# Tokens-first operands of the delta and GLA heads: from TensorE transposes to VectorE block transposes and a pass through DRAM

## The chip, the cores and the metric

The kernel runs on one core of a Trainium2 chip. The metric is the device time of one launch in microseconds (us). A core has a TensorE (PE, matmuls; PEld are its weight loads), a VectorE (DVE), a ScalarE (ACT), a GpSimd (POOL) and a SyncE (SP). SP computes nothing here; it issues most of the DMAs, in order, one after the other. All engines run their own instruction stream in order and wait for each other through semaphores.

## The reference

One inference step of two layers over 320 token columns: 256 prompt tokens (one sequence) and 64 sample tokens (8 sequences of 8), model width 2048, all in float32.

```python
# layer 0, per token: one input projection, split into the parts below
proj = x @ w_in
qkv, b_raw, a_raw, z_a, q_b, k_b, v_b, lr_b, z_b = split(proj)
qkv = silu(causal_conv(qkv, width 4))                 # delta heads: 8 heads, 128 wide
q_a = l2norm(q_a) * 128 ** -0.5;  k_a = l2norm(k_a)
beta = sigmoid(b_raw);  g = -exp(a_log) * softplus(a_raw + dt_bias)
# gated delta rule, in chunks (kb = beta * k, G = cumsum g, decay = exp(G_i - G_j))
A   = strict_lower((kb @ k.T) * decay)
sol = solve(A + I, [v * beta, kb * exp(G)])           # unit lower triangular
v_new = u - w @ S;  o = (q * exp(G)) @ S + ((q @ k.T) * decay) @ v_new
S = S * exp(g_last) + (k * exp(g_last - G)).T @ v_new
# GLA: 4 heads (128 keys, 256 values): S_t = diag(exp(gk_t)) S_{t-1} + k_t v_t^T, o_t = S_t^T q_t
x = x + (concat(norm(o_a) * silu(z_a), norm(o_b) * silu(z_b))) @ w_out
# layer 1: x = x + (RG-LRU(conv4(x w_x)) * silu(x w_g)) @ w_out ; then a final rmsnorm
```

The outputs are the tokens of both groups and the new recurrent states.

## The kernel before

**The dense stream.** All large projections are one stream of 30 groups. A group makes 512 output features in four PSUM accumulators `acc`; it runs over 8 weight chunks `wst` of 512 KB (2 slices of the depth each). Every float32 product is three matmuls on rounded parts: `xh*wh`, `xl*wh`, `xh*wl`. I call such a set of three a product; a group has 64 of them. ACT makes `wh` from `wst` (L246), DVE makes `wl` (L247), SP loads `wst` (L212) into three buffers. Features lie on the partitions, tokens on the columns.

Groups 0 to 5 are the delta heads' Q, K, V, V, K, Q (two halves of four heads each; conv taps on DVE, silu on ACT, into tiles `qkv`), 6 to 9 the GLA's q, k, v, v (tiles `gp`), 10 to 13 the gates, then the output projection and layer 1.

**The side work.** What the heads need beside the stream is written as generators in queues `hi`, `lo`, `lo2`, `tails`. After each product `slot()` advances each queue by one `yield`; a table `WAITS` says how many yields lie between two pieces. A scheduler of the language then orders the instructions of each engine by its own costs, so the place of a piece in an engine's stream is not exactly where the generator emitted it. Mentions of order below are of that final stream.

**The delta heads.** A *quad* is four heads over 128 tokens. There are four prompt quads (two halves of the heads, two chunks) and one of the sample tokens. `quad_a` prepares a quad, and it needs k, q and v with tokens on the partitions:

- it turns k, q and v with TensorE, four 128x128 transposes each (L716 `kt`, L725 `qt`, L767 `vt`; `ident` is the identity);
- ACT takes the sums of squares of k and q from PSUM (`junk`, `ss`), POOL and DVE make `nb` (minus beta over the squared norm of k) and `bk`;
- `df`, `gr` (L751) sum gates, ACT makes `dtm` (decay), PE makes `kk` (L773) and `kq` (L785), DVE multiplies them with `dtm` to `bt` and `mt`;
- `nb` is needed along columns too: PE turns it (L795 `nbt`), ACT copies it, POOL writes it to DRAM, ACT's queue reads it back as `bn`.

Then comes the inverse of the triangular matrix: `bt`'s 32x32 diagonal blocks go through DRAM (`bd_scratch`, `ab`), POOL multiplies `ab` by `bn` (L823) and solves (`invert32`, 62 instructions L828 and L830), the results return through `xd_scratch` as `XT` and `xc`. `quad_front` joins blocks (`lp`, `lxt`, `xp` scaled by `nb`), `quad_b` applies the inverse (`y`), makes the output `po` and the state `sn`. The sample quad has 8x8 blocks and inverts on DVE (`invert`); it reads the old states as `st`.

**GLA.** `gla_head` turns two blocks of v and one of k per chunk with TensorE (L1438, L1439 `gvt`), and ACT copies the three from PSUM (`gvk`).

Of the kernel before, what the change touches and what calls it, by code (L numbers as in the profile page):

```python
# [72 lines left out]
def hybrid_step(ctx, tc, x_cols, x_rows, w_head, w_dense, w_small, w_lr, w_gate, par_a, par_b, par_c, gains, last_gain,  # L73
# [9 lines left out]
    nb_d = nc.dram_tensor("nb_scratch", (20, P), F32, kind="Internal").ap()  # L83
# [3 lines left out]
    xt_d = nc.dram_tensor("xt_scratch", (4, P, P), F32, kind="Internal").ap()  # L87

# [25 lines left out]
    hi, lo, lo2, tails = [], [], [], []  # L114
# [27 lines left out]
    def slot0(n_lo=1):  # L142
        advance(hi)
        for _ in range(n_lo):
            advance(lo)
        advance(lo2)
        advance(tails)

# [397 lines left out]

    def evac_conv_a(slot_name, half, part):
# [53 lines left out]
        def after():  # L601
# [3 lines left out]
            if part == 0 and half == 1:  # L605
                hi.append(later(lambda: lo.extend([delta_half(1), delta_sample()])))
        evac.late = late
# [3 lines left out]
    def small_group():  # L611
        acc = bank("smacc")
        for k in range(KT):
            j = 32 * (k % 4)
            pe.matmul(acc[j:j + 32, :NT], smw[:, k, :], ob[k // 4][:, k % 4, :], start=(k < 4), stop=(k >= KT - 4),
                      tile_position=(0, j))
        dve.tensor_mul(sm[:, :NT], acc[:, :NT], rb0)
# [63 lines left out]
    def quad_prompt(half, c):  # L681
# [10 lines left out]
        q.late = c > 0  # L692
        q.on_tag, q.nbuf = "lg", 2
        return q

    def quad_sample():
# [9 lines left out]
        q.late = True  # L706
        q.on_tag, q.nbuf = "bt", 1
        return q

    def quad_a(q, ws, nbuf):  # L710
        U = q.U
        t = lambda nm, shape=[P, 4, P], bufs=nbuf, tag=None: ws.tile(shape, F32, name=nm, tag=tag or nm, bufs=bufs)
        ss = t("ss", [P, 8])
        ps = bank4("kt")
        for u in range(U):
            pe.transpose(ps[:, u, :], q.k(u), ident)  # L716
        q.ktm = t("ktm")
        act.activation(q.ktm, ps, AF.Copy)
        for u in range(U):
            j = t("junk", [P, P], 1)  # L720
            act.activation(j, ps[:, u, :], AF.Square, accum_out=ss[:, u:u + 1])
        yield from wait("quad_a.1")
        ps = bank4("qt")
        for u in range(U):
            pe.transpose(ps[:, u, :], q.q(u), ident)  # L725
        for u in range(U):
            j = t("junk", [P, P], 1)
            act.activation(j, ps[:, u, :], AF.Square, accum_out=ss[:, 4 + u:5 + u])
        q.bk = t("bk", [P, 4])
        q.nb = t("nb", [P, 4])  # L730
        q.nbe = t("nbe", [P, 4])
        sk = ss[:, 0:4]
        pool.tensor_scalar(sk, sk, EPS, None, op0=OP.add)
        pool.tensor_tensor(q.bk, sk, mhalf[:, :4], OP.pow)
        pool.tensor_mul(q.bk, q.bk, beta[:, q.gc:q.gc + 4])
# [8 lines left out]
        yield from wait("quad_a.2")  # L744
        dve.reciprocal(q.nb, sk)
        dve.scalar_tensor_tensor(q.nb, q.nb, -1.0, beta[:, q.gc:q.gc + 4], op0=OP.mult, op1=OP.mult)
# [13 lines left out]
        dve.tensor_mul(dt, dt, q.um[:, None, :].to_broadcast([P, 4, P]))  # L760
        q.eq = ss[:, 4:8]
        dve.tensor_scalar(q.eq, q.eq, EPS, EPS * P, op0=OP.add, op1=OP.mult)
        dve.tensor_mul(q.nbe, q.nb, es[:, q.gc:q.gc + 4])
        yield from wait("quad_a.3")
        ps = bank4("vt")
        for u in range(U):
# [1331 lines left out]
```

## Time and profile before

| | |
|---|---|
| median of 3 runs | 978.75 us (977.84 to 979.34) |
| span of the profiled execution, first to last instruction | 976.7 us |
| the median less that span | 2.05 us |
| busy: PE, DVE, ACT, POOL | 965.7, 695.6, 532.6, 193.4 us |
| PE idle for an operand: largest rows | 1.4 us (`frs`, the end), 1.2 us (`got`), 0.4 and 0.2 us (first weights) |
| mean DMA rate over the span | 179 GB/s |

The page records no time of the profiled execution apart from its span; the span and the median differ by what lies around the first and last instruction. In a row, the busy time is the sum over instructions, "mean ns" is the length of one from its start to its modelled end; matmuls overlap, so the distance between two starts is shorter than the length.

### The profile page before, as it was taken

How to read it: one execution, taken by the hardware profiler on the slowest of the kernel's cores; microseconds unless marked ns; L12 is line 12 of the kernel's file. 1: busy time of each engine (PE TensorE's matmuls, PEld its weight loads, DVE VectorE, ACT ScalarE, POOL GpSimd, SP SyncE). 2: the span in 40 equal slices, each digit the busy share in tenths (PEclk: the TensorE clock that was granted, in tenths of full speed). 3: DMA queues.
4: the chain of work that ended last, by engine and by line, in shares of the span. 5: the costliest groups of instructions: out<-in, count | busy, mean ns of one | idle time of the engine just before them, and what ended most of it. 6: DMA issues, size and time to landing. Idle time of an engine off the chain costs nothing.

```text
span 976.7 us, 18827 instructions
## 1 busy us (share of the span) xinstructions
PE 965.7 (99%) x6945; PEld 949.2 (97%) x6945; DVE 695.6 (71%) x1464; ACT 532.6 (55%) x1088; POOL 193.4 (20%) x343
## 2 busy tenths in 40 slices
PE   9999999999999999999999999999999999999996
PEld 9999999999999999999989999999999999999996
DVE  7498887666545556788658789667969668876763
ACT  7666865447333454866423345348685885333442
POOL 3010128303381011120106124100010000042200
PEclk9999999999999999999999999999999999999998
DMA  9854445534455376444578887655445445678752
GB/s 321 292 176 123 134 131 155 166 109 121 150 154 150 98 235 215 130 125 130 180 251 265 245 246 249 211 154 151 157 117 189 131 127 171 189 229 253 264 168 108
DMA packets 68125, 175.06 MB, mean 179 GB/s; under 512 B 17116, under 2 KB 26096, under 8 KB 67520
## 3 DMA queue, kind: packets, MB, share of 16 engines
q1 hardware_dynamic: 62904, 163.69, 54.5%
q0 software_dynamic: 2720, 8.66, 2.5%
q10 hardware_dynamic: 2408, 1.49, 0.5%
q8 instruction: 55, 0.90, 0.4%
q14 instruction: 38, 0.31, 0.1%
HBM read 159.14 MB, written 14.68 MB: 178 GB/s over the span
## 4 chain that ended last, share of the span: by engine, by line
PE 96%; DVE 2%; issue 0%; DMA 0%; ACT 0%; SPq 0%; POOL 0%; DVEq 0%; ACTq 0%; POOLq 0%
PE acc L380 82%; PE acc L266 3%; PE fbt L309 1%; PE gpo L1495 0%; PE lg L1683 0%; PE lg L1682 0%; PE lg L1684 0%; PE kq L785 0%; PE kk L773 0%; DMA wst<-in_w_head_dram 0%; PE gsn L1259 0%; PE po L971 0%; PE pq L1059 0%; PE sn L1245 0%; PE y L962 0%
## 5 line engine op out<-in xcount | busy, mean ns | idle before, releaser
L380 PE MATMUL acc<-xh,wh 128*128 128x320 f32 x1856 | 579.9, 313 | 0.4 <-ACT wh L233 0.4
L380 PE MATMUL acc<-xl,wh 128*128 128x320 f32 x1856 | 574.0, 310 | 0.0
L380 PE MATMUL acc<-xh,wl 128*128 128x320 f32 x1856 | 573.0, 309 | 0.2 <-DVE wl L247 0.2
L246 ACT ACTIVATE wh<-wst 128x512 fp32r<-128x512 f32 x479 | 279.2, 624 | 301.1 <-PE acc L380 259.5
L247 DVE TENSOR_TENSOR wl<-wst,wh 128x512 fp32r<-128x512 f32 x479 | 333.4, 726 | 150.6 <-ACT wh L246 149.6
L380 PEld LDWEIGHTS acc<-xh,wh 128*128 128x128 f32 x1856 | 348.6, 188 | 3.3 <-issue 1.3
L380 PEld LDWEIGHTS acc<-xl,wh 128*128 128x128 f32 x1856 | 348.6, 188 | 1.1
L380 PEld LDWEIGHTS acc<-xh,wl 128*128 128x128 f32 x1856 | 348.2, 188 | 0.9 <-DVE wl L247 0.4
L588 DVE SCALAR_TENSOR_TENSOR yc<-slab,pa,yc 128x344 f32<-128x344 f32 x72 | 40.6, 576 | 2.8 <-ACT yc L102 2.4
L830 POOL TENSOR_TENSOR xi<-xi,tmp 128x60 f32<-128x60 f32 (+24 forms) x62 | 25.9, 418 | 4.9
L828 POOL TENSOR_TENSOR tmp<-ab,xi 128x60 f32<-128x60 f32 (+24 forms) x62 | 25.1, 404 | 4.8
L1711 POOL MEMSET aa<- 128x32 f32 x4 | 0.6, 161 | 117.7 <-ACT rr L1698 66.7
L1140 POOL TENSOR_TENSOR uvkh<-uvk,uvkh 32x256 fp32r<-32x256 f32 (+1 forms) x8 | 10.8, 1344 | 51.5 <-DVE uvkh L1136 50.6
L1249 DVE SCALAR_TENSOR_TENSOR ust<-ust,es,sn 128x128 f32<-128x128 f32 x64 | 18.2, 338 | 2.8 <-PE sn L1245 2.0
L1145 POOL TENSOR_TENSOR uvm<-uvh,rm 96x512 fp32r<-96x512 f32 x16 | 19.5, 1242 | 2.8 <-PE sn L1245 2.4
L885 POOL TENSOR_TENSOR so<-so,mhalf 128x4 f32<-128x4 f32 x4 | 4.4, 1106 | 74.2 <-DVE so L884 74.2
L266 PE MATMUL acc<-xl,wh 128*128 128x320 f32 (+1 forms) x64 | 18.7, 292 | 0.0
L266 PE MATMUL acc<-xh,wl 128*128 128x320 f32 (+1 forms) x64 | 18.7, 292 | 0.0
L266 PE MATMUL acc<-xh,wh 128*128 128x320 f32 (+1 forms) x64 | 18.6, 291 | 0.0
L592 ACT ACTIVATE qkv<-yc 128x256 f32<-128x256 f32 x24 | 10.0, 415 | 15.8 <-DVE yc L588 15.6
L1263 DVE SCALAR_TENSOR_TENSOR ugt<-ugt,ebs,gsn 128x256 f32<-128x256 f32 x32 | 14.1, 474 | 5.6 <-PE gsn L1259 5.5
L1642 DVE SCALAR_TENSOR_TENSOR yc<-slab,pb,yc 128x344 f32<-128x344 f32 x32 | 17.5, 572 | 0.6 <-ACT yc L1640 0.5
(464 smaller groups left out, 1057.1 us busy)
## 6 DMA issues: line engine op xcount, KB each, us to landing
wst<-in_w_dense_dram SPq DMA_DIRECT2D x237, 512.0 KB, 4.0
st<-in_state_delta_dram SPq DMA_DIRECT2D x8, 512.0 KB, 6.3
st<-in_state_gla_dram SPq DMA_DIRECT2D x4, 1024.0 KB, 6.9
ust<-in_state_delta_dram SPq DMA_DIRECT2D x8, 512.0 KB
out_s_delta_dram<-ust POOLq DMA_DIRECT2D x8, 512.0 KB, 5.1
ugt<-in_state_gla_dram SPq DMA_DIRECT2D x8, 512.0 KB, 5.6
out_s_gla_dram<-ugt POOLq DMA_DIRECT2D x8, 512.0 KB, 4.2
xtok<-in_x_rows_dram SPq DMA_DIRECT2D x6, 512.0 KB, 5.4
```

Of the source, the lines that this page charges most:

```text
L246: act.activation(h, wst[i][:, a, :], AF.Copy)
L247: env["last_split"] = dve.tensor_sub(l, wst[i][:, a, :], h.bitcast(F32))
L266: mm = pe.matmul(accs[f][:, cols], w[:, fs], x[:, cols], start=(k == 0 and j == 0), stop=(k == KT - 1 and j == 2), skip_group_check=True)
L380: mm = pe.matmul(o, (h, h, l)[j][:, fs], (xh, xl, xh)[j][k], start=(k == 0 and j == 0), stop=(k == KT - 1 and j == 2))
L588: dve.scalar_tensor_tensor(y[:, :n], xp[:, j:j + n], pa[:, ft, j:j + 1], y[:, :n], op0=OP.mult, op1=OP.add)
L828: behind(pool.tensor_mul(tv, ab[:, j, j + 1:, None].to_broadcast([P, m, w]), xi[:, j:j + 1, :w].to_broadcast([P, m, w])))
L830: behind(pool.tensor_add(xi[:, j + 1:, :w], xi[:, j + 1:, :w], tv))
L1140: pool.tensor_sub(o, t[rows, :, cols], o.bitcast(F32))
L1145: pool.tensor_mul(m, src.bitcast(F32)[:, None, :].to_broadcast([R, 4, P]), rm4[:R, :, None].to_broadcast([R, 4, P]))
L1249: dve.scalar_tensor_tensor(s_, s_, es[:, col:col + 1], ps[:, b, :], op0=OP.mult, op1=OP.add)
L1263: dve.scalar_tensor_tensor(s_, s_, ebs[:, h, 4 * hb + b + i:4 * hb + b + i + 1], ps[:, i * 256:(i + 1) * 256], op0=OP.mult, op1=OP.add)
L1642: dve.scalar_tensor_tensor(y[:, :n], xp[:, j:j + n], pb[:, ft, 2 + j:3 + j], y[:, :n], op0=OP.mult, op1=OP.add)
```

## The change

1. Delta k, q and v are no longer turned on TensorE. `turn` lets DVE transpose 32x32 blocks of a whole `qkv` tile (four instructions of 128x256, or 128x128 for the sample tokens) into an `ob` tile, reading every fourth column; SP writes the tile to DRAM (`tp_scratch`, `ts_scratch`), and `load_turned` reads a quad's operand in one DMA with tokens on the partitions (`kin`, `qin`, `rv`). A new queue `turns` holds this work. It is done once per tile, in the groups after the tile is made.
2. `ACT` copies `kin` into `ktm` and takes the squares from SBUF. In half 0 v arrives late, in half 1 q; a generator `rest` in `lo2` fetches the late operand, and `delta_half` holds its `quad_front` until it is there.
3. `nb` stays on partitions: it is multiplied into `dtm` (four instructions per quad in place of one). The transposes `nbt`, the DRAM trip of `nb`, the POOL product L823 and the scaling by `nb` in `quad_front` go; there the copies `xp` are split between DVE and ACT.
4. The blocks of both quads of a half go out together (4 transfers in place of 8) and come back in 5 in place of 10. `bt` of the two quads is one tile.
5. The sample quad loads its first two states after the blocks of its inverse, and the next two after the first `pq`.
6. GLA's v is turned the same way (`gvv`); only k is turned on TensorE.
7. The `WAITS` numbers are changed around all of this.

```diff
-    "small_work.1": 0, ... "quad_a.1": 2, "quad_a.2": 8, ... "quad_a.7": 9, "invert32.1": 18,
+    "small_work.1": 0, ... "quad_a.1": 10, "quad_a.2": 2, ... "quad_a.7": 2, "delta_half.2": 4, "invert32.1": 12,
...
+    def turn(src, d, flag, to, gate):
+        while gate not in env["done"]:
+            yield
+        n = src.shape[2] // P
+        to = to.rearrange("p f t -> p (f t)")[:, :4 * P * n].rearrange("p (c x) -> p c x", c=n)
+        for f in range(4):
+            behind(dve.transpose(to.rearrange("p c (b u j) -> p u c b j", u=4, j=32)[:, f],
+                                 src[:, f, :].rearrange("p (c i b) -> p c b i", c=n, b=4)))
+            yield from wait("turn.1")
+        yield from wait("turn.2")
+        behind(sp.dma_start(d.rearrange("c p x -> p c x"), to))
+        yield from wait("turn.3")
+        env["done"].add(flag)
+
+    def load_turned(out, d, c=0):
+        sp.dma_start(out.rearrange("p a u j -> p a (u j)"), d[c].rearrange("(a i) (b x) -> (i b) a x", a=4, b=4))
...
     def quad_a(q, ws, nbuf):
-        ps = bank4("kt")
-        for u in range(U):
-            pe.transpose(ps[:, u, :], q.k(u), ident)
-        q.ktm = t("ktm")
-        act.activation(q.ktm, ps, AF.Copy)
...
-        ps = bank4("qt")
-        for u in range(U):
-            pe.transpose(ps[:, u, :], q.q(u), ident)
...
+        kin = rows("kin", "mt")
+        load_turned(kin, *turned(1))
+        late = {0: 2, 1: 0}.get(half)
+        if late != 0:
+            qin = q.bt.rearrange("p u (a j) -> p u a j", j=32)
+            load_turned(qin, *turned(0))
+        if late != 2:
+            q.rv = rows("rv")
+            load_turned(q.rv, *turned(2))
...
-        dve.tensor_mul(dt, dt, q.um[:, None, :].to_broadcast([P, 4, P]))
+        q.ktm = t("ktm")
+        act.activation(q.ktm.rearrange("p u (a j) -> p a u j", j=32), kin, AF.Copy)
...
+        for u in range(U):
+            dve.scalar_tensor_tensor(dt[:, u, :], dt[:, u, :], q.nb[:, u:u + 1], q.um, op0=OP.mult, op1=OP.mult)
...
-        ps = bank4("vt")
-        for u in range(U):
-            pe.transpose(ps[:, u, :], q.v(u), ident)
-        q.rv = t("rv")
-        scaled4(q.rv, ps, q.bk, NA0)
...
-        ps = bank("nbt")
-        pe.transpose(ps[:4, :P], q.nb, ident)
-        nbt = t("nbt", [4, P], 1)
-        act.activation(nbt, ps[:4, :P], AF.Copy)
-        pool.dma_start(nb_d[q.id:q.id + 4, :], nbt)
...
     def invert32(ws, first):
-        act.dma_start(bn, bass.AP(tensor=nb_d.tensor, ...))
-        pool.tensor_mul(ab, ab, bn[:, None, :].to_broadcast([P, n, n]))
...
     def delta_sample():
+            yield from quad_a(q, ws, 1)
+            inverse = invert(ws, 4, 8)
+            next(inverse)
+            yield from wait("delta_sample.9")
             load(0)
             load(1)
-            yield from quad_a(q, ws, 1)
-            yield from invert(ws, 4, 8)
+            yield from inverse
...
     def gla_head(h, ws, vt):
-            for hf in range(2):
-                vt = 2 * h + hf
-                pe.transpose(pt[:, hf, :], env["VB", vt // 4][:, vt % 4, cs], ident)
-            pe.transpose(pt[:, 2, :], kd[128][:, cs], ident)
+            pe.transpose(pt[:, :P], kd[128][:, cs], ident)
```

How the streams change is shown at three places. The first is PE where `quad_a` of the first half stands, in group 3. Before, each quad brings its own block of turns and products:

```order
L751 MATMUL df<-ug,sl_r 128x512 x2
L767 MATMUL vt<-ident,qkv 128x128 x4
L773 MATMUL kk<-qkv 128x128 x4
L785 MATMUL kq<-qkv 128x128 x4
L795 MATMUL nbt<-ident,nb 4x128
L380 MATMUL acc<-xh_116,wh 128x320
```

In the changed kernel the same place on PE holds no turn, and both quads' products follow each other:

```order
L788 MATMUL df<-ug,sl_r 128x512
L788 MATMUL gr<-ug,ones_r 128x512
L382 MATMUL acc<-xl_132,wh 128x320
L382 MATMUL acc<-xh_116,wh 128x320
L382 MATMUL acc<-xh_117,wh 128x320
L382 MATMUL acc<-xl_133,wh 128x320
L382 MATMUL acc<-xh_117,wl 128x320
L825 MATMUL kk<-qkv 128x128 x4
L832 MATMUL kq<-qkv 128x128 x4
L825 MATMUL kk<-qkv 128x128 x4
L832 MATMUL kq<-qkv 128x128 x4
```

The turns are gone, and with them the `kt` and `qt` blocks 16 to 20 products earlier; nothing else is added to PE's stream.

The second is DVE at the same moment, up to the first evacuations of group 3 (`slab`). Before:

```order
L742 TENSOR_TENSOR ug<-umask,gth 128x512
L742 TENSOR_TENSOR ug<-umask,gtl 128x512
L760 TENSOR_TENSOR dtm<-dtm,umask 128x512
L111 TENSOR_TENSOR rv<-vt,bk 128x256
L775 TENSOR_TENSOR bt<-kk,dtm 128x512
L788 TENSOR_TENSOR mt<-kq,dtm 128x512
L760 TENSOR_TENSOR dtm<-dtm,umask 128x512
L958 TENSOR_TENSOR eg<-eg,qkv 128x512
L247 TENSOR_TENSOR wl<-wst,wh 128x512 x2
L479 TENSOR_TENSOR slab<-acc,rb_84 128x256
```

In the changed kernel, with the last block transposes of V ahead of it:

```order
L558 STREAM_TRANSPOSE ob_137<-qkv 128x8x32
L249 TENSOR_TENSOR wl<-wst,wh 128x512 x2
L776 TENSOR_TENSOR ug<-umask,gth 128x512
L776 TENSOR_TENSOR ug<-umask,gtl 128x512
L816 SCALAR_TENSOR_TENSOR dtm<-dtm,nb,umask 128x128 x6
L826 TENSOR_TENSOR bt<-kk,dtm 128x512
L816 SCALAR_TENSOR_TENSOR dtm<-dtm,nb,umask 128x128
L835 TENSOR_TENSOR mt<-kq,dtm 128x512
L1006 TENSOR_TENSOR eg<-eg,qkv 128x512
L249 TENSOR_TENSOR wl<-wst,wh 128x512
L481 TENSOR_TENSOR slab<-acc,rb_84 128x256
```

Eight short products with `nb` take the place of two long ones, and the scaling of v moves elsewhere.

The third is SP at the sample quad. Before, the states come first, and the inverse's transfers follow between weight loads:

```order
L1028 DMA st<-in_state_delta_dram 128x1024 x4
L212 DMA wst<-in_w_dense_dram 128x1024
L1117 DMA kt_scratch<-ktm 4x32x128
L782 DMA bt_scratch<-bt 128x4x128
L848 DMA ab<-bt_scratch 16x8x8 x4
L865 DMA xt_scratch<-ab 16x8x8 x4
L874 DMA XT<-xt_scratch 128x4x128
L1028 DMA st<-in_state_delta_dram 128x1024 x2
```

In the changed kernel three turned operands and the states stand ahead of the inverse's block, and two state loads ahead of its result `XT`:

```order
L568 DMA kin<-ts_scratch 128x4x128
L568 DMA bt<-ts_scratch 128x4x128
L568 DMA rv<-ts_scratch 128x4x128
L1089 DMA st<-in_state_delta_dram 128x1024
L1089 DMA st<-in_state_delta_dram 128x1024 x3
L829 DMA bt_scratch<-bt 128x4x128
L562 DMA tp_scratch<-ob_139 128x2x512
L214 DMA wst<-in_w_dense_dram 128x1024
L905 DMA ab<-bt_scratch 16x8x8 x4
L920 DMA xt_scratch<-ab 16x8x8 x4
L1089 DMA st<-in_state_delta_dram 128x1024 x2
L924 DMA XT<-xt_scratch 128x4x128
```

One weight load, not shown, stands between the two rows of states; the next one is behind `bt_scratch`, which waits for a product that needs `kin`.

More of the change, by code (lines that the diff above doesn't have):

```diff
@@ L147, in slot0 @@
         advance(tails)
+        advance(turns)
     def drain(queue):
@@ L606, in after, with turned @@
                 hi.append(later(lambda: lo.extend([delta_half(1), delta_sample()])))
+            def turned():
+                if part or half:
+                    turn_conv(part, half, ob[1], "x0")
+                if part == 1 and half == 0:
+                    turn_conv(0, 0, ob[0], "x0")
+                if half:
+                    turn_sample(part)
+            hi.append(later(turned))
         evac.late = late
@@ L712, in quad_a @@
         t = lambda nm, shape=[P, 4, P], bufs=nbuf, tag=None: ws.tile(shape, F32, name=nm, tag=tag or nm, bufs=bufs)
+        half, c = q.at
+        turned = lambda part: (tp_d[2 * part + half], c) if q.n == 32 else (ts_d[part], 0)
         ss = t("ss", [P, 8])
-        ps = bank4("kt")
-        for u in range(U):
-            pe.transpose(ps[:, u, :], q.k(u), ident)
-        q.ktm = t("ktm")
-        act.activation(q.ktm, ps, AF.Copy)
-        for u in range(U):
-            j = t("junk", [P, P], 1)
-            act.activation(j, ps[:, u, :], AF.Square, accum_out=ss[:, u:u + 1])
-        yield from wait("quad_a.1")
-        ps = bank4("qt")
-        for u in range(U):
[L725 to L735, printed above, removed]
+        rows = lambda nm, tag=None: t(nm, [P, 4, 4, 32], tag=tag)
+        kin = rows("kin", "mt")
+        if q.n < 32:
+            q.bt = t("bt")
+        load_turned(kin, *turned(1))
[6 more added lines that the diff above has]
+            load_turned(q.rv, *turned(2))
         if q.n == 32:
@@ L789, in quad_a, with rest @@
         else:
-            half = lambda x, e: x.rearrange("p u (q e x) -> p (u q) e x", e=2, x=16)[:, :, e, :]
+            side = lambda x, e: x.rearrange("p u (q e x) -> p (u q) e x", e=2, x=16)[:, :, e, :]
             for e in range(2):
-                dve.tensor_mul(half(q.mt, e), half(ps, e), half(dt, 1 - e))
+                dve.tensor_mul(side(q.mt, e), side(ps, e), side(dt, 1 - e))
         yield from wait("quad_a.6")
-        ps = bank("nbt")
-        pe.transpose(ps[:4, :P], q.nb, ident)
-        nbt = t("nbt", [4, P], 1)
-        act.activation(nbt, ps[:4, :P], AF.Copy)
-        pool.dma_start(nb_d[q.id:q.id + 4, :], nbt)
-        yield from wait("quad_a.7")
+        w0 = 20 + q.gc if q.n == 32 else 36
+        dve.tensor_mul(q.nw, q.nb, es[:, w0:w0 + 4])
+        if late != 2:
+            v_scale()
+        def rest():
+            while ("t", late, half) not in env["done"]:
+                yield
+            x = rows("rv") if late else rows("qin", "pt")
+            load_turned(x, *turned(late))
+            yield from wait("quad_a.8")
+            if late:
+                q.rv = x
+                v_scale()
+            else:
+                q_sums(x)
+            env["done"].add(("rows", q.id))
+        if late is not None:
+            lo2.append(rest())
     def diag_ap(d, first, n_units, n):
@@ L992, in delta_half @@
             qs = [quad_prompt(half, c) for c in range(2)]
+            us = slice(8 * half, 8 * half + 8)
+            blocks = [slice(32 * b, 32 * b + 32) for b in range(4)]
+            bt = ws.tile([P, 8, P], F32, name="bt", tag="bt")
+            for c, q in enumerate(qs):
+                q.bt = bt[:, 4 * c:4 * c + 4]
             yield from weave(*[quad_a(q, ws, 2) for q in qs])
+            yield from wait("delta_half.2")
+            for b, bs in enumerate(blocks):
+                sp.dma_start(bd_d[us, b].rearrange("u j i -> j u i"), bt[bs, :, bs])
             env["done"].add(("a", half))
@@ L1008, in delta_half @@
             yield from wait("quad_b.1")
+            for q in qs:
+                while ("rows", q.id) not in env["done"]:
+                    yield
             yield from quad_front(qs, z[:, :, :64], z[:, :, 64:], pt, xt, xc)
@@ L1053, in delta_sample @@
                 yield from wait("delta_sample.2")
+                if pr:
+                    yield from wait("delta_sample.3")
                 pq = bank4("pq")
```

144 lines of the change are left out of this document (82 added, 62 removed), and 10 rows, old and new, of the table WAITS.

## The prediction

> **What bounds the kernel now.** I read the page's busy shares, its slices and its chain first, then the groups by shape, and then the order of time around each piece that the change touches.
>
> ```profile
> PE 965.7 (99%) x6945; PEld 949.2 (97%) x6945; DVE 695.6 (71%) x1464; ACT 532.6 (55%) x1088; POOL 193.4 (20%) x343
> PE   9999999999999999999999999999999999999996
> DVE  7498887666545556788658789667969668876763
> PE 96%; DVE 2%; issue 0%; DMA 0%; ACT 0%; SPq 0%; POOL 0%; DVEq 0%; ACTq 0%; POOLq 0%
> L380 PE MATMUL acc<-xh,wl 128*128 128x320 f32 x1856 | 573.0, 309 | 0.2 <-DVE wl L247 0.2
> L246 ACT ACTIVATE wh<-wst 128x512 fp32r<-128x512 f32 x479 | 279.2, 624 | 301.1 <-PE acc L380 259.5
> L247 DVE TENSOR_TENSOR wl<-wst,wh 128x512 fp32r<-128x512 f32 x479 | 333.4, 726 | 150.6 <-ACT wh L246 149.6
> ```
>
> PE is in every slice but the last, and 96% of the chain that ends last lies on it. Its third matmul of a product waited 0.2 us for `wl` in the whole span. ACT in turn waited 259.5 us for PE to give back `wh` buffers: the two engines that feed PE are ahead of it and stand still because of it. So PE's own instruction stream sets the time, and what an instruction costs there is the distance from its start to the next start, not its length in the row. For dense matmuls the chain gives it:
>
> ```profile
> 128.39 64.68 PE acc L380 x441
> ```
>
> 64.68 us for 441 matmuls is 0.147 us each, 0.44 us a product, though the row above says 309 ns.
>
> **The change, part by part: what leaves PE.** The groups with `ident`, and their starts in the order of time:
>
> ```profile
> L716 PE MATMUL kt<-ident,qkv 128*128 128x128 f32 x16 | 2.2, 272 | 0.0
> L725 PE MATMUL qt<-ident,qkv 128*128 128x128 f32 x16 | 2.4, 272 | 0.0
> L767 PE MATMUL vt<-ident,qkv 128*128 128x128 f32 x16 | 2.4, 272 | 0.0
> L795 PE MATMUL nbt<-ident,nb 128*4 128x128 f32 x5 | 1.4, 272 | 0.0
> L1438 PE MATMUL gvt<-ident,gp 128*128 128x128 f32 x16 | 3.1, 276 | 0.0
> ```
> ```profile
> 110.88 0.60 PE L716 MATMUL kt<-ident,qkv 128*128 128x128 f32 x4
> 111.23 0.39 PE L380 MATMUL acc<-xh,wh 128*128 128x320 f32 x1
> 111.46 0.31 PE L380 MATMUL acc<-xl,wh 128*128 128x320 f32 x1
> 111.61 0.31 PE L380 MATMUL acc<-xh,wl 128*128 128x320 f32 x1
> 111.75 0.60 PE L716 MATMUL kt<-ident,qkv 128*128 128x128 f32 x4
> ```
> ```profile
> 124.09 0.27 PE L795 MATMUL nbt<-ident,nb 128*4 128x128 f32 x1
> 124.12 0.39 PE L380 MATMUL acc<-xh,wh 128*128 128x320 f32 x1
> 124.35 0.31 PE L380 MATMUL acc<-xl,wh 128*128 128x320 f32 x1
> ```
> ```profile
> 417.51 0.39 PE L1438 MATMUL gvt<-ident,gp 128*128 128x128 f32 x2
> 417.74 0.27 PE L1439 MATMUL gvt<-ident,k 128*128 128x128 f32 x1
> 417.77 0.39 PE L380 MATMUL acc<-xh,wh 128*128 128x320 f32 x1
> 418.00 0.31 PE L380 MATMUL acc<-xl,wh 128*128 128x320 f32 x1
> ```
>
> From one `kt` block to the next are 0.87 us with one product inside (0.44), so four turns cost 0.43 us. There are five quads with three such blocks each (the rows above hold the four prompt quads, 16 instructions a row; the sample quad's are alike): 15 x 0.43 = 6.5 us. An `nbt` with the matmul after it takes 124.35 - 124.09 = 0.26 us, of which the matmul is 0.147: 0.11 us, five times, 0.6 us. Three `gvt` take 418.00 - 417.51 - 0.147 = 0.34 us, 0.115 each; 16 of the 24 go: 1.8 us. Together 81 turns, 8.9 us off PE. Nothing is added to PE: the streams of both kernels differ by these 81 instructions, and by where the rest stands.
>
> **What is added elsewhere.** DVE gets 32 block transposes of 256 columns and 12 of 128, reading every fourth column. The nearest rows:
>
> ```profile
> L910 DVE STREAM_TRANSPOSE xz<-xc 32x256 f32<-32x256 f32 x4 | 1.7, 430 | 0.1
> L1599 DVE TENSOR_REDUCE sq<-sq 128x320 f32<-128x1280 f32 x3 | 7.4, 2462 | 0.3
> L1700 DVE SCALAR_TENSOR_TENSOR th<-rr,th 128x1280 f32<-128x1280 f32 x4 | 6.0, 1490 | 1.4 <-ACT rr L1698 1.4
> 60.00:80.00 20.00, 20.00 (x151) 17.73 (x151) 18.43 (x54) 14.28 (x30) 3.53 (x8) 1.00 0.49 144
> 80.00:100.00 20.00, 19.90 (x138) 19.64 (x138) 16.00 (x40) 12.63 (x21) 0.00 (x0) 1.00 0.45 132
> 100.00:120.00 20.00, 20.00 (x143) 19.97 (x142) 17.11 (x36) 17.19 (x57) 3.60 (x6) 1.00 0.49 135
> L760 DVE TENSOR_TENSOR dtm<-dtm,umask 128x512 f32<-128x512 f32 x4 | 2.8, 691 | 1.0 <-ACT dtm L759 1.0
> L955 DVE SCALAR_TENSOR_TENSOR rv<-ks,nbe,rv 128x128 f32<-128x128 f32 x8 | 2.2, 343 | 0.1
> ```
>
> The lower end is the transpose without such a stride, 0.43 us for 256 columns (0.22 for 128). The upper end takes the ratio of a reduction that reads across a stride to a contiguous operation of the same 1280 elements, 2462 / 1490 = 1.65: 0.71 us (0.36). That is 16 to 27 us in all, and I take the lower end, since the row is the same instruction. A rule speaks against that choice: the Trainium skill ("SBUF — State Buffer", "Door 1: The DMA port swizzle", the note on SBUF "cachelines") says that lines are of 16 bytes and that an access crossing into a new line pays, and every fourth float32 is a new line each time. By that rule it is nearer to 27 us than to 16; no row here shows such a transpose, the sum on PE is the same by both, and it weighs in the chance of the second case below.
>
> DVE is idle 281 us of the span (976.7 less 695.6), so on the average there is room. It is scarce in the windows above (the third number after the stretch is DVE): 18.4, 16.0 and 17.1 of 20 us, the conv taps; the eight transposes of K and Q of half 0 fall there, 3.4 us. What hides them is the lead of the weight splits; if that goes, the evacuation of `acc` is late next, and PE stands at the next group's first product. One place is worth a sum: where `quad_a` stands before the end of groups 3 and 7, eight products with `nb` of 0.34 us (like `rv<-ks`) replace two of 0.69 and two scalings of 0.42, so DVE comes to the evacuations 0.5 us later, and `kk` stands three products (1.3 us) closer to the group's end. PE did not wait there before; 0 to 1.8 us a half, and I take 0: the largest wait of a dense matmul for DVE in the rows above is 0.2 us, nearer to that end. ACT loses ten scalings of v, five copies `nbt` and two thirds of each `gvk`, and gains six small copies; POOL loses two products of `ab` with `bn`. Neither is on the chain: nothing.
>
> **SP.** 30 transfers are added: 11 stores of turned tiles and 19 loads. 18 smaller ones go, since both quads share a block transfer. SP is one queue, and weights stand behind whatever waits in it. How long a hold is harmless is shown before:
>
> ```profile
> 122.44 0.33 SPq L212 DMA_DIRECT2D wst<-in_w_dense_dram  x1
> 125.20 4.89 SPq L780 DMA_DIRECT2D bd_scratch<-bt  x8
> 131.88 0.35 SPq L212 DMA_DIRECT2D wst<-in_w_dense_dram  x1
> ```
>
> Two weight loads were 9.4 us apart while the blocks waited for `bt`, against 3.5 us that PE takes for a chunk (24 matmuls), and `acc` has no idle row from it. In the prompt halves the changed queue waits in the same place for the same product; nothing. In the sample quad the hold is new: behind one weight load the next waits for `kin` to land, for its copy, four squares, the small DVE steps, four products with `nb`, `bt`. I estimate 11 us from rows of this page (a landing of 6.3 us as for `st`, then about 5 us of instructions of 0.3 to 0.7 us), 1.6 us above what is shown harmless.
>
> The sample's inverse is also the tightest chain, and two state loads of 512 KB now stand ahead of its result:
>
> ```profile
> st<-in_state_delta_dram SPq DMA_DIRECT2D x8, 512.0 KB, 6.3
> 354.26 0.38 SPq L782 DMA_DIRECT2D bt_scratch<-bt  x1
> 368.71 0.38 SPq L874 DMA_DIRECT2D XT<-xt_scratch  x1
> L1070 PE MATMUL y<-rv,XT x8: 270/275/348, 373.9 to 388.9; 128*128 128x128 f32 x8
> ```
>
> Before, `y` starts 5.2 us after `XT` is issued, without waiting. In the changed order `y` stands 42 products behind `kk` instead of 40, 0.9 us more room; `XT` is issued later by the state loads and lands behind 1 MB. Lower end: it still lands in time, 0. Upper end: the 6.3 us landing of such a state load less the 2.3 us by which it is longer than the 4.0 us of a weight load, that is 4.0 us. I take 1 us, nearer the lower end since 5.2 us are there to lose.
>
> **The sum.** -8.9 on PE, +1.0 at the sample's `y`: -7.9. The profiled span of 976.7 becomes 968.8; with the 2.05 us between that span and the median of the runs (978.75) the time is 970.8 us. A change within 0.2% (976.8 to 980.7) could not be told from none.
>
> **Rivals.**
>
> *A new wait takes back half (973 to 976.8).* DVE's excess in the tap groups delays evacuations, or the sample chain waits its 4 us and the hold on SP its 1.6. That is up to 5.6 us of 8.9, 975.5 us; with the 1.8 us before a group's end on top it is out of this case. For it: 18.4 of 20 us on DVE, the upper end of the stride, and a chain that goes through DRAM. Against it: holds of 9.4 us that PE did not notice.
>
> *No change (within 0.2%).* DVE becomes the bound. Between 60 and 120 us it is busy 51.5 of 60 us; 24 transposes at 0.71 us put there would make 68.5, 8.5 us too many, and 8.9 us become 0.4: 978.35 us. In the order only the eight of K and Q stand there, so it takes three times the upper price.
>
> *Slower.* One mechanism: the one SP queue. Five quads each hold the weights until a turned operand has gone to DRAM, come back and been used. A hold of 9.4 us is known to be harmless; from 11.2 us in every quad, 1.8 us too long each, the 8.9 us are gone, and at 11.9 us the time is 978.75 - 8.9 + 5 x 2.5 = 982.4. For it: the 11 us estimated for the sample quad, and the order places such loads ahead of weights in all five quads. Against it: in four of the five the operands are stored tens of products before they are loaded.
>
> *Turns cost their length.* The Trainium skill ("TensorE: Matmul & The Clock Gate", "Part 4: PE-mode transpose") gives about 275 ns for a turn in a kernel's context. The rows say 272 ns as length, but 0.11 us from start to start. Were the length what leaves, 81 x 0.272 = 22 us would go: 956.7 us. The chain's pitch speaks against it.
>
> **How the numbers follow.** Forecast (967.5 to 973) 0.63; half taken back 0.17; no change 0.10; slower 0.08; length of turns 0.02. Faster by over 0.2%: 0.63 + 0.17 + 0.02 = 0.82. The likeliest gives 970.8 us. The low end is the forecast without any new wait, 969.9, less the 1.4 and 1.2 us that PE waited in the page's two largest idle rows, 967.3; the high end is just beyond the second case, 977.5. Outside are 0.18 or so.
>
> **What the profile after would show.** Right: no `kt`, `qt`, `vt`, `nbt` rows, PE's idle rows still under 2 us each, PE still 99% busy, the span near 969, `STREAM_TRANSPOSE` of 128x256 near 0.43 us. The sample's `y` would have an idle row for `XT` of 0 to 4 us. Wrong: idle rows at `acc` for `wl`, `wh` or for an evacuation in 60 to 130 us; weight loads more than 10 us apart with PE idle behind them; or a pitch of dense matmuls above 0.147 us while DVE and the new transfers use SBUF.

## Result, and the profile after

The changed kernel takes 986.49 us (median of 4 executions, 983.52 to 987.66) against 978.3 us: the ratio is 1.0078, with a 95% interval of 1.0062 to 1.0094. It is 0.8% slower, where 0.8% faster was forecast. Busy shares, slices, chain and the first of the dense matmuls in the page of the changed kernel (the execution of 983.52 us, span 981.8):

```profile
PE 959.8 (98%) x6864; PEld 942.1 (96%) x6864; DVE 713.4 (73%) x1521; ACT 525.6 (54%) x1075; POOL 187.5 (19%) x336
PE   9999999999999998999999999999999999999997
PE 59%; DVE 2%; DMA 1%; issue 1%; ACT 1%; POOL 0%; SPq 0%; DVEq 0%; ACTq 0%; POOLq 0%
L382 PE MATMUL acc<-xh,wh 128*128 128x320 f32 x1856 | 580.1, 313 | 1.8 <-DVE smpvb L1351 1.7
```

The 81 turns are gone (6945 to 6864), and PE is still 98% busy. But the chain that ends last lies on it for 59% of the span instead of 96%: that chain now leaves PE again and again. PE's waits:

```profile
PE df L788 <- DVE ug L776: 4.9, 2, 3.5
PE y L1141 <- DMA XT<-xt_scratch: 1.9, 1, 1.9
PE got L1376 <- DVE gon L1372: 1.8, 3, 0.8
PE acc L382 <- DVE smpvb L1351: 1.7, 1, 1.7
PE ot L1172 <- DVE on L1167: 1.5, 1, 1.5
...
PE y L1010 <- DVE rv L1002: 0.9, 1, 0.9
PE lxt L973 <- issue: 0.8, 1, 0.8
```

Columns are the sum, how many times, and the longest. Of these, before had only two `got` waits of 0.6 us. Without those 1.2 us the rows make 12.2 us, all before 510 us; behind that both kernels run in step. Their last long stretch of dense matmuls starts 6.02 us later (before, then after, from the chain):

```profile
937.66 23.02 PE acc L266 x180
```
```profile
943.68 23.02 PE acc L268 x180
```

The longest wait costs more than itself. Order of time on PE, and two stretches of 4 us (PE, PEld, DVE, ACT and POOL busy, granted clock, DMA share, GB/s):

```profile
121.27 0.31 PE L382 MATMUL acc<-xh,wl 128*128 128x320 f32 x1
125.03 0.80 PE L788 MATMUL df<-ug,sl_r 128*128 128x512 f32 x1 [3.46 <-DVE ug L776]
...
127.44 0.47 PE L382 MATMUL acc<-xh,wl 128*128 128x320 f32 x1
127.71 0.47 PE L382 MATMUL acc<-xh,wh 128*128 128x320 f32 x1
```
```profile
124.00:128.00 4.00, 2.96 (x9) 2.58 (x10) 2.87 (x8) 3.17 (x8) 1.12 (x3) 0.62 0.55 140
128.00:132.00 4.00, 4.00 (x36) 4.00 (x35) 3.05 (x8) 0.50 (x2) 0.00 (x0) 0.95 0.39 146
```

Behind 3.46 us of idleness the granted clock is 0.62, and dense matmuls start 0.27 us apart instead of 0.147, until 128.5: another 1.85 us (the excess of all starts between 121 and 129 over their usual distance, less 3.46). So 14.1 us were lost, 6.02 less 0.4 from the first 15 us came out, and the difference, 8.5 us, is what the turns gave. The other executions were longer still, at a lower mean clock: 0.997 in 983.52 us, 0.993 in 986.26, 0.995 in 986.71, 0.992 in 987.66. As an estimate from these figures, 0.002 to 0.005 of the clock over 983 us is 2 to 5 us, the size of the 2.7 to 4.1 us by which they are longer. (In the traces of all these kernels the 20th product starts between 14.9 and 17.3 us, whatever the change; single traces are therefore compared behind that point.)

Why `ug` is late: DVE in the order of time, and ACT.

```profile
120.79 0.63 DVE L558 STREAM_TRANSPOSE ob<-qkv 128x256 f32<-128x256 f32 x1
...
121.46 0.62 DVE L558 STREAM_TRANSPOSE ob<-qkv 128x256 f32<-128x256 f32 x1
...
123.08 1.29 DVE L249 TENSOR_TENSOR wl<-wst,wh 128x512 fp32r<-128x512 f32 x2 [0.18 <-ACT wh L248]
124.30 0.68 DVE L776 TENSOR_TENSOR ug<-umask,gth 128x512 fp32r<-128x512 f32 x1
```
```profile
117.75 0.31 ACT L807 ACTIVATE junk<-bt 128x128 f32<-128x128 f32 x1 [2.24 <-DMA bt<-tp_scratch]
...
122.44 1.13 ACT L248 ACTIVATE wh<-wst 128x512 fp32r<-128x512 f32 x2
```

Both quads of a half make `ug` in one buffer, so the second can be made only when `df` of the first has run (120.06 to 120.70). DVE then has two turns of V (1.2 us), small steps on the sums (0.9 us) and a pair of `wl` (1.2 us) ahead of it. That pair waits 0.18 us for `wh`, which ACT reached late because its squares of q waited 2.24 us for the turned operand to come back from DRAM. So most of the 3.6 us until `ug` (124.30) is DVE's own work in its order, and little of it a wait. In the kernel before there was the same one buffer, but PE had work between the two `df`:

```profile
121.41 0.62 PE L751 MATMUL df<-ug,sl_r 128*128 128x512 f32 x2
121.87 0.60 PE L767 MATMUL vt<-ident,qkv 128*128 128x128 f32 x4
122.30 1.06 PE L773 MATMUL kk<-qkv 128*128 128x128 f32 x8
123.19 1.06 PE L785 MATMUL kq<-qkv 128*128 128x128 f32 x8
...
124.72 0.73 PE L751 MATMUL df<-ug,sl_r 128*128 128x512 f32 x2
```

From the first `df` to the second are 3.3 us there. In the changed order two products (0.88 us) stand between them, since `vt` and `nbt` are gone and `kk` and `kq` wait for turned rows, and the second `df` comes due after 1.5 us. Two things meet here: the second `df` is due 1.8 us earlier behind the first, and `ug` is made 3.3 us later behind it (4.24 us against 0.92, from 121.41 to 122.33, in the kernel before).

### The profile page after: what moved, and what is told of

Read it like the earlier page. It is cut to its first block, busy times and chain, and to the rows that moved or that the text cites. A ratio compares the mean times of both kernels' runs of the same rounds, so it can differ in the third digit from the quotient of the medians.

```text
span 981.8 us, 18705 instructions
## 1 busy us (share of the span) xinstructions
PE 959.8 (98%) x6864; PEld 942.1 (96%) x6864; DVE 713.4 (73%) x1521; ACT 525.6 (54%) x1075; POOL 187.5 (19%) x336
## 4 chain that ended last, share of the span: by engine, by line
PE 59%; DVE 2%; DMA 1%; issue 1%; ACT 1%; POOL 0%; SPq 0%; DVEq 0%; ACTq 0%; POOLq 0%
PE acc L382 51%; PE acc L268 3%; PE fbt L311 1%; DMA wst<-in_w_dense_dram 1%; DMA XT<-xt_scratch 0%; PE gpo L1566 0%; PE lg L1754 0%; PE lg L1753 0%; PE lg L1755 0%; PE gsn L1327 0%; PE sn L1313 0%; PE ga L1497 0%; DVE wl L249 0%; PE ga L1494 0%; PE got L1376 0%
## 5 line engine op out<-in xcount | busy, mean ns | idle before, releaser
L249 DVE TENSOR_TENSOR wl<-wst,wh 128x512 fp32r<-128x512 f32 x479 | 328.5, 715 | 133.6 <-ACT wh L248 127.5
L1331 DVE SCALAR_TENSOR_TENSOR ugt<-ugt,ebs,gsn 128x256 f32<-128x256 f32 x32 | 14.1, 474 | 5.6 <-PE gsn L1327 5.5
L481 DVE TENSOR_TENSOR slab<-acc,rb 128x256 f32<-128x256 f32 x36 | 15.0, 416 | 3.1 <-PE acc L382 2.7
```

Of the source, the lines that this page charges most:

```text
L249: env["last_split"] = dve.tensor_sub(l, wst[i][:, a, :], h.bitcast(F32))
L481: dve.tensor_mul(xp[:, 3:259], xp[:, 3:259] if acc is None else acc[:, :256], rb[:, :256])
L1331: dve.scalar_tensor_tensor(s_, s_, ebs[:, h, 4 * hb + b + i:4 * hb + b + i + 1], ps[:, i * 256:(i + 1) * 256], op0=OP.mult, op1=OP.add)
```

## Experiments

**First four: GLA alone, the buffer, the cover, the stride.**

*gla_only* is the kernel before with GLA's part of the diff (`turn`, the queue `turns`, `load_turned`, `gla_head`) and nothing else.

> Kernel before, with GLA's part of the change alone: v of the GLA heads turned by VectorE, 16 of the 24 gvt turns gone, two stores and four loads of turned tiles added; the delta heads as before. Theory (turns leave PE at 0.11 us each, the loss lies in the delta heads): 1.8 us faster than before, 976.0 to 977.0, no new idle row at PE. Rival (the turned operands themselves cost, by DVE's eight extra transposes and the SP queue): 978 to 981, with idle rows at acc or ga.

Measured: 984.0 us (981.7 to 985.4), ratio 1.0054 (1.0040 to 1.0068): neither expectation. The turns did give what was said (each block of four moved PE ahead by 0.44 us between 752 and 896 products), but there were two waits of 2 us and one of 1.2 (`ot`), none at `acc` or `ga`:

```profile
PE y L1094 <- DMA XT<-xt_scratch: 2.2, 1, 2.2
PE gvt L1510 <- POOL gvs L1509: 2.0, 1, 2.0
```

The first is in the sample's delta heads, which the edit does not touch; behind it the clock was 0.68 in the 4 us from 380 us. The second is a copy into a tile that, with 8 KB of turned v ahead of it in memory, came to lie where the state `gS` was still being sent out: POOL stood 3.9 us for that transfer ahead of `gvs`.

*ug_two*:

```diff
-            ug = ws.tile([P, 2, 4, P], F32R, name="ug", tag="ab", bufs=1)
+            ug = ws.tile([P, 2, 4, P], F32R, name="ug", tag=("ab", "XT")[c], bufs=1)
```

> Changed kernel, with the second prompt quad's ug in a buffer of its own (the later XT's) instead of the one that both quads share. Theory (df of the second quad waits because ug is made again in a buffer that df of the first quad has only just left, with 0.44 us of PE's work between them where there were 2.85): the waits of 3.46 and 1.46 us at df go, and the slow matmuls of 1.8 us behind the first; 980 to 981 against 986.5 of the changed kernel. Rival (DVE comes late because of the turns and of the chain that waits on DRAM, whatever the buffer): ug or dtm stays late, df or kk waits 2 to 5 us all the same, 984 to 986.

Measured: 980.44 us, 1.0022 (1.0012 to 1.0032), 6.0 us less than the changed kernel by one buffer. Both waits at `df` and the slow stretch are gone. (The expectation counts 0.44 us of PE's work between the two `df`; the trace has two products, 0.88.) A part of the wait moved on, to ACT's exponent behind the same squares:

```profile
PE y L1141 <- DMA XT<-xt_scratch: 2.0, 1, 2.0
PE kq L832 <- ACT dtm L796: 1.9, 1, 1.9
```

*cover_off* is the kernel before with `"quad_a.3": 0` made 2.

> Kernel before, with the two quads' second steps two yields later, so that df of the second quad follows df of the first with two products between them (0.9 us) and without the vt, kk, kq and nbt in between (2.85 us). Nothing else is changed: no turn by VectorE, no added transfer. Theory (the missing cover alone makes the wait): df waits 1.5 to 3.5 us in half 0 and 0.5 to 1.5 in half 1, time 980 to 984. Rival (the added transposes and transfers make it): no wait over 0.5 us at df, 978 to 979.

Measured: 984.17 us, 1.0056 (1.0044 to 1.0069), but `df` waited 0.26 us, not 1.5 to 3.5. The time lies at the theory's upper end and its mechanism did not come: with no turned operand about, DVE remakes `ug` nearly within the 0.9 us left. What was late instead was again `XT` (1.1 us). Of the 5.7 us by which its profiled span is longer, 1.6 lie in the first 15 us and 2.7 in idle rows; 1.4 us are in no row that I can name, and stay open.

*turn_flat* is the changed kernel with one letter pair exchanged in `turn`; the operands then hold their columns in another order, and its outputs are not those of the reference:

```diff
-                                 src[:, f, :].rearrange("p (c i b) -> p c b i", c=n, b=4)))
+                                 src[:, f, :].rearrange("p (c b i) -> p c b i", c=n, b=4)))
```

> Changed kernel, with VectorE's transposes reading consecutive columns instead of every fourth; the turned operands then hold the columns in another order, so the values differ. Theory (the loss is order, not DVE's load): a transpose of 256 columns falls from 0.62 to about 0.43 us, 7 to 8 us of DVE's busy time go, the wait at df stays at 2.5 us or more and the time within 1.5 us of the changed kernel's 986.5. Rival (DVE's load by the stride makes it late): the waits at df fall under 1 us and the time to 980 to 982.

Measured: 984.75 us, 1.0075 (1.0062 to 1.0088); `df` waited 2.5 and 1.0 us. The groups of turns, changed kernel and this one:

```profile
L558 DVE STREAM_TRANSPOSE ob<-qkv 128x256 f32<-128x256 f32 x24 | 14.9, 629 | 0.0
```
```profile
L558 DVE STREAM_TRANSPOSE ob<-qkv 128x256 f32<-128x256 f32 x24 | 10.1, 430 | 0.0
```

The stride is a price on DVE (0.63 against 0.43 us), and not the reason of the loss: the ratio is 1.0075 against 1.0078, and the medians are 1.7 us apart. With the shorter turns DVE stands 0.43 us for ACT's squares and 0.18 for `wh` ahead of `ug`, so the way through DRAM and ACT is not far behind DVE's own work.

**Next four: the late XT, a first mending, and stalls made on purpose.**

*ug_st* and *gla_st* are ug_two and gla_only with the later state loads held behind `XT` on SP:

```diff
+                    if u > 1:
+                        tc.add_manual_dep(i.ins, sts["xt"].ins.name, ... reason="issue_after")
```

> The kernel of ug_two, with the sample's four later state loads issued on SP behind the load of XT instead of two of them ahead of it. Theory (XT lands late because two loads of 512 KB stand ahead of it in the queue): the wait of 1.97 us at the sample's y goes or falls under 0.5, time 978.0 to 979.0 against 980.4 of ug_two. Rival (the DRAM trip of the inverse is too long by itself): the wait stays over 1.5 us and the time at 980 to 981.

> The kernel of gla_only, with the later state loads issued behind the load of XT as in ug_st. In gla_only PE waited 2.17 us for XT and its granted clock fell to 0.68 behind it, though GLA's turns have nothing to do with that chain. Theory (GLA's part only moved the two state loads ahead of XT in the built order): the wait at y and the drop of the clock go, time 979 to 980.5 against 984.0. Rival (the turned tiles' DMA traffic and DVE's extra work slow that chain): over 1.5 us of wait stays, 982 to 984.

Measured: ug_st 982.01 us, 1.0032 (1.0020 to 1.0044), and the wait for `XT` grew to 2.9 us. The theory falls. In place of the two loads, two stores (`kt_scratch`) and a weight load now stand ahead of `XT`, so it is issued 20.6 us behind `kk` instead of 19.7; and the program's builder put `y` nearer, due 22.2 us behind `kk` instead of 22.8. gla_st 980.88 us, 1.0016 (1.0006 to 1.0027), 0.4 us above its theory: nothing named `XT` is left at `y` (1.2 us for `wl` instead), but `gvs` took 2.8 us, and behind it the clock was 0.50 for 3.4 us.

*mended* is ug_st with five counts of the table of waits moved (`quad_a.1` 10 to 9, `quad_a.2` 2 to 3, `quad_b.1` 23 to 25, `quad_b.5` 3 to 4, `delta_sample.7` 4 to 6).

> The kernel of ug_st, with five counts of the table of waits moved so that each remaining wait gets room: the second step of a quad's start 10 to 9 and the third 2 to 3 (df and its exponent earlier, kk where it was), the front of the inverse 23 to 25, the product with the state 3 to 4, the sample's turn back 4 to 6. Theory (turns are worth 8 us on PE, and the rest are waits for lead that was taken away): idle rows at kq, lxt, y, acc and ot under 0.5 us each, 971 to 975. Rival (DVE, ACT and DMA have too little room for the turned operands, and waits only move): idle rows of 5 us or more in all before 450 us, 976 to 980.

Measured: 982.47 us, 1.0035 (1.0022 to 1.0047). The rival held in its rows (10.5 us of idleness between 15 and 450 us), and the time lies even above its range: against ug_st `kq` fell from 2.2 to 0.9, and `smpvb`, which had no row there, took 3.1 us. The counts say when a step is written; the builder then places it by its own estimate.

*stalls* is the kernel before with `dve.tensor_reduce(pad, ident[:, :4, None].to_broadcast([P, 4, P * r]), ...)` at eight places, r from 8 to 22.

> Kernel before, with one long sum added on VectorE at eight places between 530 and 830 us, of about 4 to 12 us in steps of 1, which makes wl late and PE stand still there for times from 0 to some 8 us; its sums are not used. Theory (a stall of over about 2 us costs more than itself, since the granted clock falls behind it): places with an idle row under 2.0 us keep the clock at 1.00, those over 2.2 us show 0.6 to 0.7 in the next 4 us and lose another 1.5 to 2 us. Rival (the clock falls only behind stalls of over 3.4 us, and the drops seen so far have another cause): stalls of 2.2 to 3.4 us leave the clock at 1.00.

Measured (one execution, 1011.48 us): idle rows of 1.26 and 1.84 us left the clock at 1.00, one of 1.86 did not, nor did those of 2.88, 3.10, 4.22 and 6.83 us. Four us behind the row of 1.26 (it ends at 609.10), and the four right behind 1.86 (643.99):

```profile
612.00:616.00 4.00, 4.00 (x30) 4.00 (x29) 4.00 (x15) 1.40 (x3) 1.57 (x4) 1.00 0.81 255
644.00:648.00 4.00, 4.00 (x17) 4.00 (x18) 3.85 (x10) 1.58 (x3) 0.00 (x0) 0.57 0.18 29
```

17 matmuls instead of 30: 1.9 us. The rival (nothing under 3.4 us) is out, and 2 us is no sharp edge; the last section has what divides them.

**Then: what each wait really stands behind.** In the sample quad of the changed kernel `kk` runs at 347.47, and its product `bt` is made 4.6 us later; before it was 1.4 us. DVE and the chain:

```profile
350.18 0.69 DVE L811 TENSOR_TENSOR rv<-rv,bk 128x512 f32<-128x512 f32 x1 [1.42 <-POOL bk L819]
...
352.02 0.69 DVE L826 TENSOR_TENSOR bt<-kk,dtm 128x512 f32<-128x512 f32 x1
...
359.71 1.29 DVE L249 TENSOR_TENSOR wl<-wst,wh 128x512 fp32r<-128x512 f32 x2 [3.61 <-ACT wh L248]
```
```profile
352.07 0.65 DVE bt L826
352.74 0.38 SPq L829
353.16 0.51 SPq L562
353.76 5.18 DMA wst<-in_w_dense_dram
359.05 0.64 ACT wh L248
359.75 0.50 issue
360.36 0.64 DVE wl L249
361.11 0.24 DVE xi L914
...
367.06 4.82 DMA XT<-xt_scratch
```

`bt` stands behind the scaling of v, which waits for POOL. The inverse on DVE (from 360.92) stands behind a `wl` whose weights were issued on SP behind the store of the blocks (L829), which waits for `bt`, and behind the 512 KB store of GLA's turned v (L562, 0.5 us in the chain). From the weight load before, issued at 344.53, to this one are 9.2 us. In gla_only the GLA store was issued at 343.51 and is not in the chain; there the builder put one more `wl` ahead of the inverse (it waited 1.9 us for `wh`, until 362.70), and evacuations ahead of its last copy, and two state loads stood ahead of `XT`. At 297 us DVE stood 4.05 us with the transposes `xz`, waiting for the inverse, ahead of the evacuations that PE then missed (`smpvb`).

*gla_clean* is gla_only with the second turn of v gated behind the sample (`"gdns" if idx else ("a", 0)`), and `gvk` and `gqm` allotted before `gvs`.

> Kernel before with GLA's part alone, as gla_only, and two things moved: the turn and the store of the second half of v come after the sample's delta heads, so that neither stands ahead of the weights and the inverse there; and the tiles gvk and gqm of the sample's GLA stage take their place in memory first, so that gvs no longer lies where the state gS still goes out. Theory (GLA's 16 turns are worth 1.8 us; gla_only lost it to the inverse behind late weights and to a tile that reused memory): no idle row over 1 us between 10 and 970 us, 976.5 to 977.5 against 978.5 of the kernel before. Rival (turned operands cost by themselves, in DVE time and DMA traffic): 979 to 981.

Measured: 976.9 us, 0.9986 (0.9977 to 0.9995): 1.6 us faster than before, as the theory had it, with no idle row over 0.61 us between 10 and 970 us. The order on DVE at the sample's inverse is that of the kernel before again. Both moves came at once, so the theory's late weights are not shown apart from that order.

*ug_order* is ug_two with that gate and the scaling of v held behind `bt` on DVE.

> The kernel of ug_two, with the scaling of v put behind the product bt on DVE's order (it waited there for POOL's bk, with dtm and bt behind it), and the second GLA turn and its store behind the sample's delta heads. Theory (XT is late because bt is made 3 us later after kk than before, and because the weights, and with them wl ahead of the inverse on DVE, stand behind a store of 512 KB): the sample's bt comes within 4 us of kk instead of 5.3, the wait for XT falls under 0.5 us, time 978 to 979 against 980.4 of ug_two. Rival (the DRAM trip of the inverse of some 8 us is too long for the room at y whatever stands ahead): the wait stays at 1.5 to 2.5 us, 980 to 981.

Measured: 977.52 us, 0.9994 (0.9983 to 1.0005). The time came, and more; `bt` was made 2.6 us after `kk`, yet `XT` still cost 1.6 us: with three state loads ahead of it, it was issued 20.0 us behind `kk`, no earlier than the 19.7 of ug_two. Mending one of two causes did not free `y`.

*mend2* is ug_order with `quad_a.1` 9, `quad_a.2` 3, and half 1's `xz` behind the first GLA v group.

> The kernel of ug_order, with df one step earlier and kk where it was (10 to 9, 2 to 3), and the transposes xz of half 1 placed on DVE behind the evacuation of the first GLA v group instead of ahead of it, where they held DVE 4.05 us for the inverse's DMA. Theory (each wait is one of order): the waits at acc for smpvb and at kq under 0.7 us, time 974 to 977. Rival (waits only move to the next place): idle rows of 5 us or more in all between 100 and 450 us, 978 to 981.

Measured: 976.61 us, 0.9986 (0.9973 to 1.0000). The theory's two waits and its time came: `smpvb` has no wait, `kq` 0.4. But `lxt` 1.8, `XT` 1.6, `ot` 1.1 and `y` 0.9 are left, and the idle rows of 7.0 us between 100 and 450 us are the rival's.

*turns_back* is the changed kernel with the delta heads' 60 turns on PE again, without their turns on DVE, stores and loads; all else as changed.

> Changed kernel, with the delta heads' 60 turns back on TensorE (k and q at the start of a quad, v behind kq) and without their VectorE turns, stores and loads; beta on partitions, the joint block transfers, the table of waits and GLA's part stay as changed. It adds 6.5 us to PE. Theory (half of the loss is the order at a quad's start, with one ug buffer and nothing between the two df): df of the second quad still waits 1 to 3.5 us, time 986 to 990. Rival (the loss is the trip of the turned operands by VectorE, DRAM and ACT's squares): waits at df and in the sample quad under 1 us each, 979 to 983.

Measured: 980.93 us, 1.0024 (1.0013 to 1.0035). Here the rival held, but for the 1.3 us at the sample's `XT`:

```profile
PE y L1121 <- DMA XT<-xt_scratch: 1.3, 1, 1.3
...
PE df L791 <- DVE ug L780: 1.0, 2, 0.6
PE y L990 <- DVE rv L982: 0.6, 1, 0.6
```

With one `ug` buffer and as little between the two `df`, they wait 1.0 us in all, not 4.9: `ug` is made 1.40 us behind the first `df` (121.32 to 122.72), where the changed kernel takes 4.24. 60 turns more on PE, some 6 us, and the kernel is 5.6 us faster by the medians: the turned operands of the delta heads cost about 12 us of waits and slowed clock. How much of it is DVE's turns and how much the way through DRAM and ACT, no run separates.

**Last: what of the waits is only place.**

*mend3* is mend2 with the state loads behind `XT`, and the sample's `y` and `ot` held in place with `delta_sample.4` 20 instead of 8. *mend4* is mend3 with half 0's front ten steps later, and its transposes `xz` held to their places too.

> The kernel of mend2, with the four later state loads behind XT on SP, and the sample's y and its turn back ot held to their places in the program, y with 20 steps of room instead of 8 (45 products behind kk, ot 19 behind y). Theory (mending the load order alone, or bt alone, let the builder move y nearer, so each alone won little; together the room suffices): the wait for XT under 0.3 us and at ot under 0.3, 2.5 us less than mend2, 973.5 to 975. Rival (the trip through DRAM takes longer than any room here): over 1 us at y stays, 976 to 978.

> The kernel of mend3, with the front of half 0's inverse ten steps later, so that lp stands at product 388 as in the kernel before instead of 375, out of the stage in which ACT and DVE evacuate a conv group. Theory (lxt and y wait since the copies of lp stand behind that group's work): the idle rows at lxt and y of half 0 under 0.5 us, 2 us less than mend3, 971 to 973.5, near the forecast of 970.8. Rival (later stages move with it and new waits of the same size come up): 974 to 977.

Measured: mend3 975.92 us, 0.9974 (0.9964 to 0.9984), faster than both kernels, by 10.6 us than the changed one; the sample's `XT` and `ot` have no row left:

```profile
PE got L1387 <- DVE gon L1383: 1.7, 3, 0.6
PE lxt L979 <- issue: 1.5, 2, 1.0
...
PE kq L834 <- ACT dtm L796: 1.3, 1, 1.3
...
PE y L1016 <- DVE rv L1008: 0.9, 1, 0.9
```

It came 0.9 us short of its expectation: `kq` took 0.9 us more than in mend2. The sample's `y` stands 45 products behind `kk` in mend2 and here alike, so it was not room but the earlier load that freed it: `XT` is issued 19.1 us behind `kk` instead of 20.4. `ot` got room, 19 products behind `y` instead of 10. mend4 983.45 us, 1.0054 (1.0041 to 1.0066): `lxt` and half 0's `y` are rid of their waits, but GLA's tiles met the outgoing state again, and behind it the clock was 0.50 for 3.4 us:

```profile
PE gvt L1565 <- POOL gvs L1564: 2.7, 1, 2.7
```

So the full 8 us were not reached: in mended and in mend4, shifting some steps brought other steps together.

## Why the prediction was wrong, by its steps

- **Turns off PE, -8.9.** Right in kind, a little large. The changed kernel's trace gives 8.5 (14.1 lost, 5.6 came out). mend3 gives 7.2: its idle rows between 15 and 960 us exceed before's by 5.5 us, and behind the start it is 1.65 ahead. gla_clean shows 1.6 of the 1.8 forecast for its 16 by the medians, with 0.5 to 2.3 as the interval; its trace is 0.85 us ahead behind the start. So 7 to 8.5.
- **DVE's turns.** I took the lower end, 0.43 us, and the row is 0.63, nearer to the upper (0.71); DVE's busy time grew by 17.8 us. The rule that I weighed against my choice, the Trainium skill's note on SBUF "cachelines" ("SBUF — State Buffer", "Door 1: The DMA port swizzle"), points the right way, and turn_flat agrees: without the stride 0.43.
- **"What hides them is the lead of the weight splits."** This is the step that failed. I asked whether `wl` or an evacuation of `acc` would be late. `wl` was not (0.2 us); one evacuation was, `smpvb` with 1.7 us, at 300 us and not in the tap groups, behind transposes that waited for the inverse's DMA. The largest loss was at `ug`, behind `wl` in DVE's order, and in it pieces that I had costed as separate and hidden: DVE's turns, its small sums, `wl` behind `wh`, and behind these ACT's squares and the DRAM trip. ug_two and turns_back show the two halves that it takes: with a second buffer, or without turned operands, `df` waits 0 or 1.0 us. The 0 to 1.8 us "before a group's end", taken as 0, stood nearest to it: the two `df` waited 4.9 us, and the clock took another 1.85. The sum had no term at all for `ot` 1.5, half 0's `y` 0.9 and `lxt` 0.8 us.
- **What the removed instructions covered.** `vt`, `kk`, `kq` and `nbt` stood between the two `df`. I counted two of them as gain and never as the work that hid the remaking of `ug`. cover_off says that this alone makes hardly a wait (0.26 us): `ug` must come late as well.
- **SP.** "In the prompt halves nothing": PE did not stand for weights there, but ACT's squares waited 2.24 us for `bt<-tp_scratch`, a load of these halves that I had priced at nothing. In the sample the hold estimated at 11 us was 9.2, and PE did not stand for those weights. But I judged a hold at PE alone. The chain to the late `XT` runs through it: `bt`, the store of the blocks, GLA's store, the weights, `wh`, `wl`, and behind `wl` on DVE the inverse. That stood in no step.
- **The sample's `y`, 0 to 4, taken as 1.** 1.9 us in the trace, inside its bounds. The reason given (loads of state ahead of `XT`) is one of two, the other being the late inverse: ug_st and ug_order each went at one and kept 2.9 and 1.6 us of wait; mend3 went at both and has none.
- **The rivals.** "Slower" had 0.08 and the sign, 982.4 us, but by the SP queue. No rival took a chain over several in-order engines. The range ended at 977.5 because I added the bounds of three places; PE waited at seven.
- **The signs named.** Idle rows "under 2 us each" became 3.46 us, the span "near 969" 981.8, the turn "near 0.43 us" 0.63. Of the signs of being wrong, a pitch above 0.147 us came (0.27), where the clock was 0.50; that traffic in SBUF had a part in it is not shown. The late evacuation came outside of 60 to 130 us.

## What to carry to other kernels

An instruction that leaves the bounding engine also leaves a gap that used to cover something: for each, ask which buffer or operand was being remade under it. When an operand goes through DRAM instead of through the bounding engine, add up its whole way over the in-order engines (landing, ACT, DVE, what stands behind them), and compare it with the products between its producer and its use, place by place. A queue that is held harms not only the engine that bounds: ask what stands behind the late operand on every engine. And find out where a step is really placed in the built order before trusting a wait count: mending one cause of two can leave the wait as it was.

## What the hardware showed that was not expected

The granted clock falls behind stalls much shorter than I had thought, and not always. Over all traces here, all nine idle rows of PE from 2.67 to 6.83 us were followed by a lower clock, which cost some 1.4 to 2.3 us each. From 1.4 to 2.6 us some were (1.43 in ug_order, 1.86 in stalls, 2.17 in gla_only, 2.55 in turn_flat) and some not (1.86 in the changed kernel, 1.97 in ug_two, 2.54 in mended). The Trainium skill ("TensorE: Matmul & The Clock Gate", "HAM oscillation — how this bites in real kernels") puts the limit at idle gaps of about 3.4 us; the rows from 1.43 to 3.10 us that lowered the clock lie below it.

What divides them shows when the stretches are cut where the clock changes. In these traces it is 1.00 or 0.50 and nothing between; a figure such as 0.62 is a mean over a window that holds both. The sixteen low stretches between 15 and 960 us last 3.41 us each (one 6.83), and each begins a whole multiple of 3.41 us behind the first change of the clock in its trace. In the 3.41 us just before, PE had been idle for 1.86 us or more in fifteen of them (1.43 in ug_order); where no low stretch followed, such a stretch held at most 1.72 us of idleness. So it is the idle time that falls into one such stretch that decides here: the 2.54 us of mended lay over two of them (1.41 and 1.13) and cost no clock, the 1.86 us of stalls lay in one. The Trainium skill (the same page, "What's actually happening" in its Part 1) calls the window that decides free-running, and these traces agree: the first change comes between 4.3 and 10.5 us, and where a wait falls against the stretches differs from trace to trace. The executions of the changed kernel, between 983.5 and 987.7 us at different mean clocks, would agree with that, but only one of them was traced.
